# The last down block ahead of each later first up product is put 128 bytes further, in a longer tile

## The chip, the cores and the metric

The kernel runs on one core of one Trainium2 chip. The metric is the device time of one execution in microseconds, taken as the median of several runs; less is better. The profile shows one execution of the same program.

## The reference

One decoder block in fp32 on a sequence of 512 tokens of width 1024, in three residual parts and a final norm:

```python
h = rms_norm(x, g_mix);  proj = h @ w_in           # pooling mixer and differential attention, gated
x = x + mixed @ w_out
hc = rms_norm(x, g_cross)
x = x + memory_cross_attention(hc, mem_n, w_cq, w_ckv, w_co)
hm = rms_norm(x, g_mlp)                             # the part that this change touches
x = x + jnp.square(jax.nn.relu(hm @ w_up)) @ w_down # w_up 1024 x 4096, w_down 4096 x 1024
return rms_norm(x, g_final)
```

## The kernel before

Everything is kept transposed: features on the 128 partitions, tokens along the free dimension. Each fp32 product is made of three float32r matmuls (`mm3`, lines 105 to 107). Weights and right operands are split into hi, a copy rounded to float32r, and lo, what is left; the three matmuls are hi by hi, hi by lo, and lo by hi. Each loads its 128x128 weights anew (PEld in the profile) while the matmul before it streams. The split of a weight block of 128x1024 is a cast on ACT (line 111) and a subtraction on DVE (line 112).

Weights come in blocks of 128x1024 (512 KB). The list `blocks` holds them in the order of use. The MLP begins at block 64 (`FIRST_UP`) and has four groups of 22 blocks:

- 14 blocks for up products, in two sets of seven. The first matrix of the MLP is multiplied by a Strassen scheme (Winograd's form): seven block products of 256 columns in place of eight. Each is 24 matmuls 256 wide, `sc<-mix,...` or `sc<-s,...`, into PSUM tile `sc`, with right operands in the tiles `mix` and `s`. The first of a set is "A11", the second "s2" (in group 0's first set "s1").
- 8 blocks for down products. Each is 24 matmuls 512 wide, `acc<-xg,...`, into `acc`, with the right operand in `xg`. DVE then adds the result to the residual (line 573).

So group g uses the blocks from 64 + 22g on, and its last down block, number 64 + 22(g + 1) - 1, stands directly ahead of A11 of group g + 1. For groups 0, 1 and 2 these are blocks 85, 107 and 129, and the A11 behind them are blocks 86, 108 and 130.

In the MLP `weights(i)` loads blocks up to seven ahead and splits up to four ahead of block i. Splits go to buffers of two kinds. Blocks whose number leaves a remainder of 3 or 4 by 5 go to the tag `mhl`, which has four buffers, two pairs of hi and lo. All others go to `whi` and `wlo`, with three each. Together that is five blocks: the one in use and four ahead. The order of PE's instructions is the program's; the other engines' order is set by a scheduler, which also hands a buffer to a new tile once its last reader is done. Unsplit blocks lie in `wraw` (three) and `mraw` (five). Loads are issued by SP, and POOL issues those that add a second part of a weight onto a first; sums of parts are also made by DVE (lines 182 and 185).

Tiles of a tag lie one behind another. Where each begins in a partition follows from the sizes. Past a multiple of 512 bytes, `whi`, `wlo`, `xg` and the all-ones matrix `ones` begin at 0, `mhl` at 256, `mix` at 64 and `s` at 320; slices within them are multiples of 512 bytes.

During the third product of group 0, the row sums for the norm of the MLP (`stats2`) put two 512-wide matmuls on `ones` between the others (lines 237 and 238).

Of the kernel before, what the change touches and what calls it, by code (L numbers as in the profile page):

```python
# [12 lines left out]
F32R = mybir.dt.float32r  # L13
# [4 lines left out]
P = 128  # L18
T = 512
D = 1024  # L20
# [5 lines left out]
NG = FF // (P * KC)  # L26
# [24 lines left out]
def block_kernel(ctx: ExitStack, tc: tile.TileContext, x0g, xT, memT, wv, wm, wst, wckv, wpool, vecs, csts, outT):  # L51
# [17 lines left out]
    def nm(s):  # L69
        uid[0] += 1  # L70
        return f"{s}_{uid[0]}"
# [4 lines left out]
    def sb(tag, shape, bufs, dt=F32):  # L76
        p = apool if tag in EARLY_TAGS else late["pool"] if tag in LATE_TAGS else pool
        return p.tile(shape, dt, tag=tag, name=nm(tag), bufs=bufs)
# [16 lines left out]
    def f(ap):  # L95
        return ap.bitcast(F32)
# [13 lines left out]
    def split(hi, lo, src, eng=V):  # L110
        S.copy(hi, src)  # L111
        eng.tensor_tensor(lo, src, f(hi), op=ALU.subtract)  # L112
# [27 lines left out]
    def add(src):  # L140
        blocks.append(src)
        return len(blocks) - 1
# [12 lines left out]
    def load(i):  # L155
        if i >= len(blocks):
            return
        if isinstance(blocks[i], tuple):
            n, name = blocks[i]
            if (n, "A11") not in raw:  # L160
                fetch((n, "A11"), part(n, "A11"), "mraw", 5)
            if (n, "s1") not in raw and name in ("s1", "s2"):
                r = fetch((n, "s1"), part(n, "A22"), "wraw", 3)
                nc.gpsimd.dma_start(r, part(n, "A21"), accum_op=ALU.add)
            if (n, "s3") not in raw and name == "s3":
                r = fetch((n, "s3"), part(n, "A21"), "mraw", 5)
                nc.gpsimd.dma_start(r, part(n, "A11"), accum_op=ALU.add)  # L167
            if name in ("A12", "A22"):
                fetch((n, name), part(n, name), "mraw", 5)
        elif i == 0 and i not in raw:  # L170
            r = raw[i] = sb("wraw", [P, D], 3)
            nc.sync.dma_start(r[:, :T], blocks[i][:, :T])
            load_x(1)
            nc.sync.dma_start(r[:, T:], blocks[i][:, T:])
        else:
            fetch(i, blocks[i], "wraw", 3)

    def combined(n, name):

        if name == "s2":  # L180
            r = raw[n, "s2"] = sb("wraw", [P, D], 3)
            V.tensor_tensor(r, raw[n, "s1"], raw[n, "A11"], op=ALU.add)
        elif name == "s4":
            r = raw[n, "s2"]
            V.tensor_tensor(r, r, raw[n, "A12"], op=ALU.add)
            return r
        return raw[n, name]

    def prep(i):
        if i >= len(blocks) or i in ready:  # L190
            return
        load(i)
        r = combined(*blocks[i]) if isinstance(blocks[i], tuple) else raw[i]
        if i >= FIRST_UP and i % 5 > 2:
            hi = sb("mhl", [P, D], 4, F32R)
            lo = sb("mhl", [P, D], 4, F32R)
        else:
            hi = sb("whi", [P, D], 3, F32R)
            lo = sb("wlo", [P, D], 3, F32R)
        if i == 0:  # L200
            V.tensor_copy(hi[:, :T], r[:, :T])
            V.tensor_tensor(lo[:, :T], r[:, :T], f(hi[:, :T]), op=ALU.subtract)
            split(hi[:, T:], lo[:, T:], r[:, T:])
        else:
            split(hi, lo, r, G if i in WPOOL else V)
        ready[i] = (hi, lo)

    def weights(i):
        far = 4 if i >= FIRST_UP else 0
        for j in range(i, i + 4 + far):  # L210
            if j < FIRST_UP or late:
                load(j)
        for j in range(i, i + 3 + far // 2):
            if j < FIRST_UP or late:
                prep(j)
        return ready.pop(i)
# [104 lines left out]
    for m in CO_ORDER:  # L321
        where["co", m] = add(wm[WCO + m])
    FIRST_UP = len(blocks)
    for g in range(NG):
        for n in (2 * g, 2 * g + 1):
            for name in FIRST_ORDER if n == 0 else ORDER:
                where[n, name] = add((n, name))
        for m in range(KC):
            where["dn", g, m] = add(wm[WDN + KC * g + m])
# [19 lines left out]
    load(0)  # L349
    x_in(0)  # L350
    prep(0)
    x_in(1)
    for k in range(2, KC):
# [568 lines left out]
    for g in range(NG):  # L922
# [3 lines left out]
        for m in range(KC):  # L926
# [4 lines left out]
            if last and m == KC - 1:  # L931
                st["sp3"] = split_sq(ss3, T)
                for hf, o in enumerate((ps("sc", 3), ps("sc", 3))):
                    c = slice(hf * M, (hf + 1) * M)
# [90 lines left out]
```

## Time and profile before

| | |
|---|---|
| median of 3 runs | 734.94 us (733.79 to 735.09) |
| profiled execution, its own time | 733.65 us |
| its span, first to last instruction | 731.7 us |
| mean granted TensorE clock | 0.987 |
| busy: PE / PEld / DVE / ACT / POOL | 706.8 / 614.1 / 512.7 / 392.4 / 72.6 us |
| HBM read / written | 86.24 / 2.10 MB |

Busy time is the time in which an engine has an instruction under way. PE is the matmuls and PEld the weight loads, which overlap them; matmuls are pipelined, so the duration of one is longer than the step from its start to the next one's. A row of the timeline gives start in us, duration in us, engine, line, operation, out<-in and shape; in brackets stands the idle time ahead of it and what ended it.

### The profile page before, as it was taken

The page shows a single profiled execution, that of the slowest core. Times are in us where ns is not written, and L with a number is a line of the kernel's source. Part 1 is how long each engine was busy: PE and PEld are TensorE (multiplying, and loading weights), DVE is VectorE, ACT ScalarE, POOL GpSimd, SP SyncE. Part 2 cuts the span into 40 slices and gives each one's busy share as a digit, 9 for nine tenths or more (in the row PEclk, how much of TensorE's full clock was granted, in tenths as well). Part 3 has the DMA queues.
Part 4 walks back from the last instruction along what each step waited for, and adds up shares of the span by engine and source line. Part 5 has one row for each costly group of instructions (what it writes and reads, how often), then busy time and mean ns, then how long its engine had stood idle before and what let it go on. Part 6 is the DMA issues. An engine that isn't in the chain of part 4 may idle for free.

```text
span 731.7 us, 10275 instructions
## 1 busy us (share of the span) xinstructions
PE 706.8 (97%) x3960; PEld 614.1 (84%) x3960; DVE 512.7 (70%) x797; ACT 392.4 (54%) x641; POOL 72.6 (10%) x66
## 2 busy tenths in 40 slices
PE   9999999999999999999969999999999999999993
PEld 6877888788889888888849988899889988899882
DVE  7597999975888555663887974588455974489426
ACT  7498998676766433543754641256214651256422
POOL 0044112534000000000000001000000001000003
PEclk9999999999999999999988999999999999999997
DMA  8433223143525542114734646265354645314003
GB/s 318 142 114 117 78 82 115 59 142 119 173 91 186 187 141 87 58 58 159 187 86 122 197 143 144 86 173 184 77 115 146 202 144 118 83 58 144 30 1 115
DMA packets 28112, 91.09 MB, mean 124 GB/s; under 512 B 3072, under 2 KB 5120, under 8 KB 28064
## 3 DMA queue, kind: packets, MB, share of 16 engines
q1 hardware_dynamic: 25712, 81.92, 33.9%
q0 software_dynamic: 2352, 8.52, 6.9%
q8 instruction: 31, 0.51, 0.3%
q14 instruction: 17, 0.14, 0.1%
HBM read 86.24 MB, written 2.10 MB: 121 GB/s over the span
## 4 chain that ended last, share of the span: by engine, by line
PE 81%; DVE 6%; DMA 5%; ACT 5%; issue 1%; POOL 0%; SPq 0%; DVEq 0%; POOLq 0%; ACTq 0%
PE acc L105 16%; PE acc L107 15%; PE acc L106 15%; PE sc L105 10%; PE sc L107 10%; PE sc L106 10%; DMA wraw<-wst 3%; DMA mraw<-wst 2%; DVE wlo L112 1%; ACT tmp L448 1%; ACT whi L111 1%; DVE mix L849 1%; DVE tmp L446 1%; DMA tmp<-xT 1%; PE sc L387 1%
## 5 line engine op out<-in xcount | busy, mean ns | idle before, releaser
L111 ACT CAST whi<-wraw 128x1024 fp32r<-128x1024 f32 (+1 forms) x98 | 102.4, 1045 | 118.1 <-PE acc L106 50.8
L105 PE MATMUL acc<-xg,whi 128*128 128x512 f32 x400 | 158.2, 396 | 0.0
L107 PE MATMUL acc<-xg,wlo 128*128 128x512 f32 x400 | 156.1, 390 | 0.0
L106 PE MATMUL acc<-xg,whi 128*128 128x512 f32 x400 | 155.8, 390 | 0.0
L112 DVE TENSOR_TENSOR wlo<-wraw,whi 128x1024 fp32r<-128x1024 f32 (+1 forms) x98 | 121.3, 1238 | 27.7 <-ACT whi L111 27.4
L107 PEld LDWEIGHTS acc<-xg,wlo 128*128 128x128 f32 x400 | 75.1, 188 | 16.1
L105 PEld LDWEIGHTS acc<-xg,whi 128*128 128x128 f32 x400 | 75.2, 188 | 15.0 <-issue 0.3
L106 PEld LDWEIGHTS acc<-xg,whi 128*128 128x128 f32 x400 | 75.2, 188 | 14.5
L573 DVE TENSOR_TENSOR vr<-acc,vr 128x512 f32<-128x512 f32 x41 | 28.3, 690 | 72.3 <-PE acc L107 72.3
L105 PE MATMUL sc<-mix,whi 128*128 128x256 f32 (+1 forms) x192 | 56.8, 296 | 0.0
L107 PE MATMUL sc<-mix,wlo 128*128 128x256 f32 (+1 forms) x192 | 56.4, 294 | 0.0
L106 PE MATMUL sc<-mix,whi 128*128 128x256 f32 (+1 forms) x192 | 56.4, 294 | 0.0
L885 DVE TENSOR_TENSOR tmp<-sc,tmp 128x512 f32<-128x512 f32 x56 | 37.7, 686 | 7.5 <-PE sc L107 7.3
L111 ACT CAST mhl<-wraw 128x1024 fp32r<-128x1024 f32 x22 | 23.2, 1053 | 35.6 <-PE acc L106 22.2
L111 ACT CAST whi<-mraw 128x1024 fp32r<-128x1024 f32 x19 | 19.9, 1050 | 38.6 <-PE acc L106 21.8
L106 PE MATMUL acc<-xg,mhl 128*128 128x512 f32 x104 | 40.6, 390 | 0.0
L105 PE MATMUL acc<-xg,mhl 128*128 128x512 f32 x104 | 40.5, 389 | 0.0
L107 PE MATMUL acc<-xg,mhl 128*128 128x512 f32 x104 | 40.5, 389 | 0.0
L105 PEld LDWEIGHTS sc<-mix,whi 128*128 128x128 f32 x192 | 36.5, 190 | 1.0
L106 PEld LDWEIGHTS sc<-mix,whi 128*128 128x128 f32 x192 | 36.4, 189 | 1.1
L107 PEld LDWEIGHTS sc<-mix,wlo 128*128 128x128 f32 x192 | 36.4, 190 | 1.1
L167 POOL DMA_DIRECT2D mraw<-wst x8 | 6.9, 864 | 263.5 <-DMA mraw<-wst 164.3
(270 smaller groups left out, 1684.9 us busy)
## 6 DMA issues: line engine op xcount, KB each, us to landing
wraw<-wm SPq DMA_DIRECT2D x76, 512.0 KB, 3.3
mraw<-wst SPq DMA_DIRECT2D x32, 512.0 KB, 3.4
wraw<-wckv SPq DMA_DIRECT2D x16, 512.0 KB, 3.4
mraw<-wst POOLq DMA_DIRECT2D x8, 512.0 KB, 5.7
wraw<-wst SPq DMA_DIRECT2D x8, 512.0 KB, 3.3
wraw<-wst POOLq DMA_DIRECT2D x8, 512.0 KB, 5.6
s<-s SPq DMA_DIRECT2D x8, 256.0 KB, 3.6
vr<-xT SPq DMA_DIRECT2D x8, 256.0 KB, 4.4
```

Of the source, the lines that this page charges most:

```text
L105: nc.tensor.matmul(o, lh, rh, start=start, stop=False)
L106: nc.tensor.matmul(o, lh, rl, start=False, stop=False)
L107: nc.tensor.matmul(o, ll, rh, start=False, stop=stop)
L111: S.copy(hi, src)
L112: eng.tensor_tensor(lo, src, f(hi), op=ALU.subtract)
L167: nc.gpsimd.dma_start(r, part(n, "A11"), accum_op=ALU.add)
L387: nc.tensor.matmul(o[i], xg[k][0][:, tb], wh[:, c], start=k == 0, stop=False)
L446: V.tensor_tensor_reduce(e[:, :n], o[:, :n], mask[:, T - n:], -0.125, 3.0e38, ALU.add, ALU.min, mn)
L448: S.activation(e[:, :n], e[:, :n], AF.Exp, bias=mn, scale=-1.0, accum_out=sm[:, c:c + 1])
L573: V.tensor_tensor(t, o, t, op=ALU.add)
L849: eng.tensor_tensor(y3[j][:, i, c], y3[j][:, i, c], r, op=ALU.mult)
L885: V.tensor_tensor(u[new], o, u[old], op=ALU.add)
```

## The change

Two things change. All four `mhl` buffers are declared 32 elements (128 bytes) longer. The blocks 85, 107 and 129 (`LAST_DOWN`) take their hi and lo from `mhl` and use its elements 32 to 1055 in place of 0 to 1023. Blocks 85 and 107 were in `whi` and `wlo` before; 129 was in `mhl` already. All other `mhl` blocks use elements 0 to 1023 of the longer buffers. No instruction is added or removed, and nothing that is computed changes.

```diff
@@ prep
-        if i >= FIRST_UP and i % 5 > 2:
-            hi = sb("mhl", [P, D], 4, F32R)
-            lo = sb("mhl", [P, D], 4, F32R)
+        if i >= FIRST_UP and (i % 5 > 2 or i in LAST_DOWN):
+            c = slice(32, 32 + D) if i in LAST_DOWN else slice(D)
+            hi = sb("mhl", [P, D + 32], 4, F32R)[:, c]
+            lo = sb("mhl", [P, D + 32], 4, F32R)[:, c]
         else:
             hi = sb("whi", [P, D], 3, F32R)
             lo = sb("wlo", [P, D], 3, F32R)
@@ the list of blocks
     FIRST_UP = len(blocks)
+    LAST_DOWN = {FIRST_UP + 22 * (g + 1) - 1 for g in range(NG - 1)}
```

## The prediction

> **What bounds the kernel now.** I read the page first: busy times, the slices, the chain by engine.
>
> ```profile
> span 731.7 us, 10275 instructions
> ...
> PE 706.8 (97%) x3960; PEld 614.1 (84%) x3960; DVE 512.7 (70%) x797; ACT 392.4 (54%) x641; POOL 72.6 (10%) x66
> ...
> PE   9999999999999999999969999999999999999993
> ...
> PE 81%; DVE 6%; DMA 5%; ACT 5%; issue 1%; POOL 0%; SPq 0%; DVEq 0%; POOLq 0%; ACTq 0%
> ```
>
> PE is busy everywhere, and the chain is PE. The second view is PE's waits, longest first:
>
> ```profile
> PE sc L105 <- ACT mix L111: 4.0, 1, 4.0
> PE sc L106 <- DVE mix L112: 3.2, 1, 3.2
> ```
>
> These two are where the MLP begins (slice 21); no longer wait of PE is listed, so within the MLP PE waits for nobody that matters. What can move there is the spacing of matmuls. So the third view is busy time by stretch; I cut it at the first matmul of each stage. A row gives the length in us, then PE's, the weight loads', DVE's, ACT's and POOL's busy time, the granted clock, the DMA share and GB/s.
>
> ```profile
> 396.82:424.02 27.20, 27.20 (x242) 27.20 (x241) 26.20 (x35) 17.77 (x24) 0.85 (x1) 1.00 0.65 184
> 467.78:507.36 39.58, 39.58 (x338) 39.58 (x336) 32.96 (x40) 22.77 (x28) 0.86 (x1) 1.00 0.56 173
> 550.91:590.49 39.58, 39.58 (x337) 39.57 (x336) 32.95 (x40) 22.77 (x28) 0.86 (x1) 1.00 0.57 173
> 634.05:673.62 39.57, 39.57 (x337) 39.57 (x336) 32.95 (x40) 22.76 (x28) 0.00 (x0) 1.00 0.28 93
> 435.14:467.78 32.64, 32.64 (x145) 27.03 (x144) 15.06 (x15) 6.32 (x7) 2.58 (x3) 1.00 0.48 113
> ```
>
> The first row is ten 256-wide up products of group 0, 240 matmuls: 27.20/240 = 113.3 ns from one to the next. The next three are all 14 up products of groups 1, 2 and 3, 336 matmuls each: 39.58/336 = 117.8 ns. Same shape, same code, same clock (1.00), PE busy throughout, yet 4.46 ns apart, and constant within each stretch. The last row is six 512-wide down products, 144 matmuls at 226.7 ns. So the up products have a quick and a slow pace, and something at the entry picks one. The fourth view, the timeline of PE, shows the entries: the only change to quick in the MLP, and an entry into slow.
>
> ```profile
> 394.20 0.28 PE L107 MATMUL sc<-mix,wlo 128*128 128x256 f32 x1
> 394.32 0.40 PE L237 MATMUL tr<-tmp,ones 128*128 128x512 f32 x1
> 394.56 0.39 PE L238 MATMUL tr<-tmp,ones 128*128 128x512 f32 x1
> 394.78 0.28 PE L105 MATMUL sc<-mix,whi 128*128 128x256 f32 x1
> 394.90 0.28 PE L106 MATMUL sc<-mix,whi 128*128 128x256 f32 x1
> 395.01 0.28 PE L107 MATMUL sc<-mix,wlo 128*128 128x256 f32 x1
> ...
> 467.55 0.39 PE L107 MATMUL acc<-xg,wlo 128*128 128x512 f32 x1
> 467.78 0.28 PE L105 MATMUL sc<-mix,whi 128*128 128x256 f32 x1
> 467.90 0.28 PE L106 MATMUL sc<-mix,whi 128*128 128x256 f32 x1
> 468.02 0.28 PE L107 MATMUL sc<-mix,wlo 128*128 128x256 f32 x1
> ```
>
> Two 512-wide matmuls on `ones` in the middle of a product (the row sums of `stats2`) turn 0.12 us steps into 0.11; a full down block ahead of A11 leaves 0.12. The pace is a state that the last wide matmuls hand on, and the change touches exactly the block that hands it on to groups 1, 2 and 3.
>
> That the place of the operands matters to spacing at all is seen in two other products, each of 24 matmuls, whose weights and right operand lie otherwise to each other:
>
> ```profile
> 249.64 0.40 PE L105 MATMUL acc<-whi,s 128*128 128x512 f32 x1
> 255.24 0.40 PE L105 MATMUL acc<-whi,s 128*128 128x512 f32 x1
> ...
> 711.74 0.28 PE L105 MATMUL sc<-xg,whi 128*128 128x256 f32 x1
> 714.61 0.28 PE L105 MATMUL sc<-xg,whi 128*128 128x256 f32 x1
> ```
>
> Tiles begin, past a multiple of 512 bytes: `whi`, `wlo`, `xg`, `ones` at 0, `mhl` at 256, `mix` at 64, `s` at 320 (from the tiles' sizes in order). With weights in `s` and the right side in `whi`, 512-wide: 5.60/24 = 233.3 ns, not 226.7. With `whi` and `xg`, 256-wide: 2.87/24 = 119.6, not 113.3 or 117.8.
>
> **The change part by part.** No instruction is added or removed.
>
> (1) *Shifted last block.* Blocks 85, 107, 129 have their weights 128 bytes further, so the A11 products of groups 1 to 3 are entered from another relation. No row has a 128-byte shift: known are 0 and 256 (down blocks from `whi` and `mhl`, equal below) and 64 (unequal above). Bounds: all three groups turn quick, 3 x 336 x 4.46 ns = 4.50 us gained; or none, 0. I take the gain. The quick pace once entered held for all ten remaining products of group 0, over every change of tile, and the slow one over 14, so the entry decides; and a block of 24 matmuls with two shifted loads out of three is a larger disturbance than the two on `ones`. Against: `ones` is itself at offset 0, so what turned the pace there was not an offset.
>
> (2) *Longer tiles.* The four `mhl` buffers are 4224 bytes apart, not 4096, so they begin at 256, 384, 0 and 128 past 512. As the buffers are handed out, every `mhl` block's hi stays on a multiple of 256 and its lo lies 128 off; in the three shifted blocks hi is off and lo is not.
>
> ```profile
> L106 PE MATMUL acc<-xg,whi 128*128 128x512 f32 x152 | 59.1, 389 | 0.0
> L106 PE MATMUL acc<-xg,mhl 128*128 128x512 f32 x104 | 40.6, 390 | 0.0
> L107 PE MATMUL sc<-mix,mhl 128*128 128x256 f32 x88 | 25.2, 287 | 0.0
> L107 PE MATMUL sc<-s,mhl 128*128 128x256 f32 x88 | 24.5, 278 | 0.0
> ```
>
> (The 287 holds a stretch at half clock at the start of the MLP.) In up products 88 + 88 = 176 lo matmuls move; in down products (104/8 = 13 blocks now, 15 after) 12 x 8 lo and 3 x 16 hi, 144. Bounds: nothing, as between 0 and 256 bytes above (389 and 390 ns each); or the dearest rows, 176 x (119.6 - 113.3) = 1.1 us and 144 x (233.3 - 226.7) = 1.0 us, 2.1 us together. A gain on the wide ones is excluded: 226.7 is the lowest spacing they show. I take 0.5 us, near the row of the nearest shift.
>
> (3) *Buffers.* Blocks 85 and 107 leave `whi`/`wlo` (three each) for `mhl` (two pairs): 85 waits for 83's pair, 109 for 107's.
>
> ```profile
> 456.92 1.05 ACT L111 CAST mhl<-wraw 128x1024 fp32r<-128x1024 f32 x1 [4.43 <-PE acc L106]
> 458.00 1.22 DVE L112 TENSOR_TENSOR mhl<-wraw,mhl 128x1024 fp32r<-128x1024 f32 x1 [0.21 <-ACT mhl L111]
> 462.34 0.39 PE L105 MATMUL acc<-xg,whi 128*128 128x512 f32 x1
> ...
> 550.89 1.05 ACT L111 CAST whi<-mraw 128x1024 fp32r<-128x1024 f32 x1 [4.34 <-PE acc L106]
> 551.11 0.69 DVE L573 TENSOR_TENSOR vr<-acc,vr 128x512 f32<-128x512 f32 x1 [3.31 <-PE acc L107]
> 551.97 1.22 DVE L112 TENSOR_TENSOR wlo<-mraw,whi 128x1024 fp32r<-128x1024 f32 x1 [0.16 <-ACT whi L111]
> 553.74 0.28 PE L105 MATMUL sc<-s,mhl 128*128 128x256 f32 x1
> ```
>
> 83 ends near 456.9, where today 88 takes its pair: 85 would be ready at 458.00 + 1.22 = 459.2 and is wanted at 462.34, 3.1 us spare. 107 ends near 550.9, where today 112 is split: 109 would be ready at 551.97 + 1.22 = 553.19, wanted at 553.74, 0.55 us spare. Behind those waits on ACT and DVE stand only later splits and the residual adds, which come first on DVE (551.11); the raw tiles of 85 and 109 are held some 16 us longer, and SP's and POOL's loads into them are wanted groups of products later. Cost 0. If ACT put one more 1.05 us cast first at 550.89, PE would wait about 0.5 us, once. Blocks 86, 87, 90, 110 to 112 get buffers sooner, which nobody awaits.
>
> The sum, against the profiled execution (731.7 span, 733.65 with what lies around it): -4.50 + 0.5 = -4.0. The median of the runs is 734.94, 1.29 above that execution; I take the change off the median: 734.94 - 4.50 + 0.5 = 730.9.
>
> **The rivals.** *No effect:* the pattern of places repeats every 128 bytes, or the pace hangs on how the last wide matmuls end and not on addresses. For it: `ones` above, and `whi` against `mhl` equal. Against: 64 bytes matter. Time 734.9.
> The Trainium skill ("TensorE: Matmul & The Clock Gate", Part 2, Step-by-step) speaks for this one: PE reads the moving operand and the next weights over two independent ports, so loading weights takes no bandwidth from a running matmul. By that rule no placement costs and the time is unchanged; the trace agrees where 389 and 390 ns stand side by side, and does not where 119.6, 117.8 and 113.3 do.
>
> *Part of the groups turn:* group 2's A11 has its weights in `mhl`, groups 1 and 3 in `whi`, so entries differ; or a `mhl` product within a group, its lo now 128 off, throws the pace back. One group quick: 734.94 - 1.50 + 0.5 = 733.9; two: 732.4.
>
> *Slower:* the lo's of the longer tiles are the wrong relation. Place: 37 `mhl` blocks. Price: up to 2.1 us, and group 0 loses its quick pace, (424.02 - 394.78)/0.1133 = 258 matmuls x 4.46 ns = 1.15 us. With no group turning that is 738.2. It decides from 1.5 us, say group 0's loss plus 50 of the 320 moved matmuls at 6.6 ns. For it: the paces above never improve on 113.3 and 226.7, and both were reached with hi and lo alike. Against: a shift of 256 costs nothing.
>
> **How the numbers follow.** 0.2% of 734.94 is 1.5 us, about what a measurement of this kernel can tell from no change. Chances: all three turn 0.36; part 0.12; no effect 0.32; slower 0.20. Faster: 0.36 and half of the partial ones, 0.42. Within 0.2%: the no-effect case and the other half, 0.38. Slower 0.20. Predicted is the likeliest, 730.9; its own range is 729.6 (all gained, nothing paid, a run 0.8 below) to 732.6 (the full 2.1 paid). The range over all reaches from 729.6 over the unchanged time to 736.7, which leaves out half of the slower case and the tail of the first.
>
> **What would show it.** Right: the up stretches of groups 1, 2 and 3 take 38.1 us each, not 39.6, with the clock at 1.00; group 0's ten products stay at 27.2; wide `mhl` products stay at 226.7 ns; no wait of PE at the first s2 of group 2. Wrong: stretches of 39.6 (no effect); stretches that change pace at a `mhl` product (partial); group 0 above 27.2 or wide products towards 233 (slower).

## The result and the profile after

| | before | after |
|---|---|---|
| median of 12 runs | 735.21 us (733.79 to 736.65) | 737.32 us (736.09 to 739.61) |
| profiled execution, its span | 731.7 us | 734.3 us |
| ratio of the times, 95% interval | | 1.0024 [1.0014, 1.0034] |

The change makes the kernel slower by 0.24%, above the range of the prediction and on the other side of its forecast. Line numbers are two higher in the changed kernel from the list of blocks on: the residual add is line 575. The rows below are of its page: the groups of the wide down products from `mhl`, with busy time, mean ns of one, and idle time ahead.

```profile
L107 PE MATMUL acc<-xg,mhl 128*128 128x512 f32 x120 | 47.7, 397 | 0.0
L106 PE MATMUL acc<-xg,mhl 128*128 128x512 f32 x120 | 47.6, 397 | 0.0
...
L105 PE MATMUL acc<-xg,mhl 128*128 128x512 f32 x120 | 46.9, 391 | 0.0
```

Before, line 106 from `mhl` took 390 ns on average; now it and line 107 take 397. The busy time by stretch of the changed kernel shows it block by block. The columns are those of the prediction.

```profile
396.41:423.61 27.20, 27.20 (x242) 27.20 (x241) 26.19 (x35) 17.50 (x24) 0.85 (x1) 1.00 0.64 182
440.24:445.68 5.44, 5.44 (x25) 4.51 (x24) 2.49 (x3) 1.05 (x2) 0.00 (x0) 1.00 0.50 87
451.12:456.67 5.55, 5.55 (x25) 4.54 (x24) 1.92 (x2) 1.03 (x1) 0.00 (x0) 1.00 0.85 189
462.22:467.83 5.61, 5.61 (x25) 4.51 (x24) 1.92 (x2) 1.08 (x2) 0.86 (x1) 1.00 0.59 93
467.83:507.57 39.74, 39.74 (x338) 39.74 (x337) 34.09 (x42) 22.77 (x28) 0.86 (x1) 1.00 0.58 173
535.02:541.24 6.22, 5.60 (x26) 4.35 (x24) 1.97 (x3) 1.82 (x2) 0.00 (x0) 1.00 0.53 84
552.40:592.13 39.73, 39.73 (x337) 39.73 (x336) 34.23 (x41) 22.72 (x28) 0.86 (x1) 1.00 0.60 173
636.18:675.89 39.71, 39.71 (x337) 39.70 (x336) 33.01 (x40) 22.77 (x28) 0.00 (x0) 1.00 0.30 93
```

- Row 1: group 0's ten up products stay quick, 27.20 us.
- Rows 2 to 4: a down block from `whi` takes 5.44 us, one from `mhl` with its lo 128 bytes off 5.55, and block 85, which is shifted, 5.61.
- Rows 5, 7 and 8: the up products of groups 1 to 3 take 39.74, 39.73 and 39.71 us, 0.14 to 0.16 more than before. None turned quick.
- Row 6: block 105 in group 2 takes 6.22 us, of which PE is busy 5.60. That is a wait, the only one that is listed within the MLP:

```profile
PE acc L105 <- DVE vr L575: 0.6, 1, 0.6
```

The timeline of PE shows where in a product the time goes (start in us, duration, engine, line):

```profile
523.92 0.39 PE L105 MATMUL acc<-xg,mhl 128*128 128x512 f32 x1
524.15 0.40 PE L106 MATMUL acc<-xg,mhl 128*128 128x512 f32 x1
524.38 0.40 PE L107 MATMUL acc<-xg,mhl 128*128 128x512 f32 x1
524.62 0.39 PE L105 MATMUL acc<-xg,mhl 128*128 128x512 f32 x1
```

Three matmuls take 0.70 us; from `whi` they take 3 x 226.7 = 680 ns. In the trace's start times in ns, the step after line 105 stays at 227, that after line 106 (during which the lo is loaded) is 232 to 233, and that after line 107 (which uses the lo) 234 to 235.

The wait has its cause on DVE. The timeline of DVE in the changed kernel around it (idle time and its releaser in brackets):

```profile
539.27 1.22 DVE L182 TENSOR_TENSOR wraw<-wraw,mraw 128x1024 f32<-128x1024 f32 x1 [7.52 <-DMA wraw<-wst]
540.41 0.68 DVE L575 TENSOR_TENSOR vr<-acc,vr 128x512 f32<-128x512 f32 x1
541.01 1.22 DVE L112 TENSOR_TENSOR mhl<-mraw,mhl 128x1024 fp32r<-128x1024 f32 x1
542.14 0.69 DVE L575 TENSOR_TENSOR vr<-acc,vr 128x512 f32<-128x512 f32 x1
```

and the same place in the kernel before:

```profile
534.79 0.69 DVE L573 TENSOR_TENSOR vr<-acc,vr 128x512 f32<-128x512 f32 x1 [3.16 <-PE acc L107]
...
540.23 0.69 DVE L573 TENSOR_TENSOR vr<-acc,vr 128x512 f32<-128x512 f32 x1 [2.10 <-PE acc L107]
...
542.39 1.22 DVE L182 TENSOR_TENSOR wraw<-wraw,mraw 128x1024 f32<-128x1024 f32 x1
```

The scheduler has put a sum of weight parts (line 182) ahead of the residual add in place of behind it. DVE stands idle for 7.52 us until a transfer lands, and behind that sum stands the add that frees the PSUM tile for PE.

Summed product by product over the MLP, up to the first narrow product behind it (711.74 us before, 714.32 after): wide `mhl` products +1.64 us; 17 narrow `mhl` products in the slow pace, 2.853 for 2.827 us each, +0.45; blocks 105 and 106 of group 2 +0.89; the second product of the MLP, whose mean granted clock was 0.91 after and 0.78 before, 3.09 for 3.54, -0.45; the start of that product +0.05. That is +2.58, the whole difference between the two profiled executions (the medians differ by 2.11). The -0.45 is not the change's: in `no_107` below, whose instructions up to there are the same in kind and order, that product took 3.62 us.

### The profile page after: what moved, and what is told of

It is laid out like the page before. It is cut to its first block, busy times and chain, and to the rows that moved or that the text cites. A ratio compares the mean times of both kernels' runs of the same rounds, so it can differ in the third digit from the quotient of the medians.

```text
span 734.3 us, 10273 instructions
## 1 busy us (share of the span) xinstructions
PE 708.4 (96%) x3960; PEld 615.0 (84%) x3960; DVE 512.1 (70%) x797; ACT 392.2 (53%) x641; POOL 72.6 (10%) x66
## 5 line engine op out<-in xcount | busy, mean ns | idle before, releaser
L111 ACT CAST whi<-wraw 128x1024 fp32r<-128x1024 f32 (+1 forms) x96 | 100.2, 1044 | 116.0 <-PE acc L106 44.4
L105 PE MATMUL acc<-xg,whi 128*128 128x512 f32 x384 | 152.2, 396 | 0.6 <-DVE vr L575 0.6
L107 PE MATMUL acc<-xg,wlo 128*128 128x512 f32 x384 | 150.0, 391 | 0.0
L106 PE MATMUL acc<-xg,whi 128*128 128x512 f32 x384 | 149.7, 390 | 0.0
L112 DVE TENSOR_TENSOR wlo<-wraw,whi 128x1024 fp32r<-128x1024 f32 (+1 forms) x96 | 119.0, 1240 | 26.4 <-ACT whi L111 26.0
L107 PEld LDWEIGHTS acc<-xg,wlo 128*128 128x128 f32 x384 | 72.1, 188 | 15.4
L105 PEld LDWEIGHTS acc<-xg,whi 128*128 128x128 f32 x384 | 72.2, 188 | 15.1 <-issue 1.0
L106 PEld LDWEIGHTS acc<-xg,whi 128*128 128x128 f32 x384 | 72.3, 188 | 13.9
L107 PE MATMUL acc<-xg,mhl 128*128 128x512 f32 x120 | 47.7, 397 | 0.0
L106 PE MATMUL acc<-xg,mhl 128*128 128x512 f32 x120 | 47.6, 397 | 0.0
L111 ACT CAST mhl<-wraw 128x1024 fp32r<-128x1024 f32 x24 | 25.3, 1053 | 41.9 <-PE acc L106 28.1
L105 PE MATMUL acc<-xg,mhl 128*128 128x512 f32 x120 | 46.9, 391 | 0.0
```

What stands on the lines that cost most here:

```text
L105: nc.tensor.matmul(o, lh, rh, start=start, stop=False)
L106: nc.tensor.matmul(o, lh, rl, start=False, stop=False)
L107: nc.tensor.matmul(o, ll, rh, start=False, stop=stop)
```

## The experiments

Three theories stood after this. *Place*: the relation of the weights' address to that of the right operand sets the step, and the longer tiles put every lo of `mhl` into a dearer one. *Order*: the move of a block changed the scheduler's order on DVE. *Pair*: the pace of the up products is turned by two wide matmuls amid narrow ones, not by an address.

### Where the time went: long_only, move_only, no_107, shift_129

`long_only` has the longer tiles alone; no block is moved or shifted.

```diff
-            hi = sb("mhl", [P, D], 4, F32R)
-            lo = sb("mhl", [P, D], 4, F32R)
+            hi = sb("mhl", [P, D + 32], 4, F32R)[:, slice(D)]
+            lo = sb("mhl", [P, D + 32], 4, F32R)[:, slice(D)]
```

> The longer mhl tiles alone: no block is moved or shifted, the buffers lie 4224 bytes apart, so that every lo in mhl begins 128 bytes off a multiple of 256. Theory of the place (a weight load 128 off costs about 6.7 ns in the matmul that it loads under and in the one that it runs in): the 13 wide mhl blocks take 5.55 us instead of 5.44 (1.4 us together), the 16 mhl up products of groups 1 to 3 2.853 instead of 2.826 (0.43 us), group 0's stay at 2.72, no wait of PE in the MLP, the whole 1.8 us slower than before. Rival, theory of the buffers (the loss comes from blocks 85 and 107 changing their buffers): no difference from before.

Measured: 736.01 against 734.15 us, ratio 1.0027 [1.0012, 1.0041]. Its groups of PE:

```profile
L107 PE MATMUL acc<-xg,mhl 128*128 128x512 f32 x104 | 41.3, 397 | 0.0
L106 PE MATMUL acc<-xg,mhl 128*128 128x512 f32 x104 | 41.3, 397 | 0.0
L105 PE MATMUL acc<-xg,mhl 128*128 128x512 f32 x104 | 40.5, 389 | 0.0
```

The 397 of the changed kernel are there, with no block shifted: 5.547 us for a wide `mhl` product, 2.853 for a narrow one in the slow pace, 2.720 still in the quick. Summed over the MLP, +1.23 wide and +0.45 narrow: 1.68 us, and no wait of PE. The longer tiles alone carry most of the loss: 1.86 us by the medians, of 2.11 for the whole change.

`move_only` moves blocks 85 and 107 to `mhl`, with tiles of the old length and no shift.

```diff
-        if i >= FIRST_UP and i % 5 > 2:
+        if i >= FIRST_UP and (i % 5 > 2 or i in LAST_DOWN):
...
```

> Blocks 85 and 107 take their buffers from mhl as in the changed kernel, but tiles keep their length and nothing is shifted. Theory of the buffers: DVE puts the sum of parts of L182 ahead of a residual add in group 2, PE waits about 0.6 us for that add and the two blocks around it take about 0.9 us more; every other product as before; the whole 0.9 us slower. Rival, theory of the place: no difference from before, and the wait goes away with the longer tiles.

Measured: 734.14 against 734.15 us, ratio 0.9997 [0.9980, 1.0014]. Wide products from `mhl` take 5.44 us again. DVE's timeline has the new order:

```profile
537.81 1.23 DVE L182 TENSOR_TENSOR wraw<-wraw,mraw 128x1024 f32<-128x1024 f32 x1 [6.63 <-DMA wraw<-wst]
538.95 0.68 DVE L575 TENSOR_TENSOR vr<-acc,vr 128x512 f32<-128x512 f32 x1
```

but blocks 105 and 106 lose only 0.13 us together (5.453 and 5.560 us), not 0.89. The order is the move's; its price depends on when the transfer lands, here 6.63 and not 7.52 us after DVE began to wait.

`no_107` is the changed kernel with block 107 left in `whi` and `wlo`.

```diff
-    LAST_DOWN = {FIRST_UP + 22 * (g + 1) - 1 for g in range(NG - 1)}
+    LAST_DOWN = {FIRST_UP + 22 * (g + 1) - 1 for g in (0, 2)}
```

> The changed kernel, but block 107 stays in whi and wlo unshifted; 85 moves and is shifted as before, and so is 129. Theory of the buffers (the wait in group 2 comes from 107's change, by which DVE's order puts L182 and its wait for a transfer ahead of a residual add): no wait of PE in group 2, its wide whi blocks all at 5.44; what remains is the cost of places, 1.8 us and twice 0.06. Rival (the wait comes from 85, or from the longer tiles): the wait of about 0.6 us is still there.

Measured: 738.77 us in one run, median of before 734.93. DVE's old order is back:

```profile
544.14 0.69 DVE L575 TENSOR_TENSOR vr<-acc,vr 128x512 f32<-128x512 f32 x1 [2.11 <-PE acc L107]
...
546.31 1.23 DVE L182 TENSOR_TENSOR wraw<-wraw,mraw 128x1024 f32<-128x1024 f32 x1
```

and with it the wait is gone: all `whi` blocks of group 2 take 5.440 us. It is the move of 107 that reorders DVE. Yet the run as a whole is slow, for three reasons that lie ahead of the first instruction that the edit changes: the MLP began 1.9 us later than in the changed kernel (377.37 for 375.46), its second product took 0.53 us longer, and group 0 stayed in the slow pace, which costs 1.25 us from the pair of `stats2` on. The last is taken up below.

`shift_129` has tiles 64 elements longer, which keeps all of `mhl` on multiples of 256 bytes, and shifts block 129 alone.

```diff
+            c = slice(32, 32 + D) if i == FIRST_UP + 65 else slice(D)
-            hi = sb("mhl", [P, D], 4, F32R)
+            hi = sb("mhl", [P, D + 64], 4, F32R)[:, c]
... (lo alike)
```

> mhl tiles are 256 bytes longer, so that all buffers begin on a multiple of 256 again, and of the last down blocks only 129 is shifted by 128 bytes, hi and lo alike; no block changes its kind of buffer. Theory of the place: block 129 takes 24 x 6.7 ns more, 5.60 us instead of 5.44, every other block as before, and the first product behind it stays slow, 2.83 us. Rival 1 (only a difference between hi and lo costs): block 129 stays at 5.44. Rival 2 (a block shifted as a whole does turn the pace): group 3's 14 up products take 2.72 us each, 38.1 in all, instead of 39.6.

Measured: 733.33 us in one run, median of before 734.15. Its busy time by stretch, for block 128, block 129 and the up products of group 3:

```profile
622.59:628.03 5.44, 5.44 (x25) 4.50 (x24) 3.14 (x3) 1.06 (x1) 0.00 (x0) 1.00 0.06 12
628.03:633.62 5.59, 5.59 (x25) 4.53 (x24) 1.92 (x2) 1.08 (x2) 0.00 (x0) 1.00 0.29 97
633.62:673.20 39.58, 39.58 (x338) 39.58 (x337) 32.95 (x40) 22.76 (x28) 0.00 (x0) 1.00 0.26 94
```

The shifted block itself pays 0.15 us, its `mhl` neighbour nothing, and the up products behind it stay at 117.8 ns. The shift alone is a small loss in the trace, too small to be seen in one run's time, and it turns nothing.

### What turns the pace: the pairs

`ones_mid` puts two 512-wide matmuls on `ones` into A11 of groups 1 to 3, after 12 of its 24; what they compute is not read.

```diff
+    def turn(again):
+        t = ps("tr", 2)
+        nc.tensor.matmul(t, ones, again[0], start=True, stop=False)
+        nc.tensor.matmul(t, ones, again[1], start=False, stop=True)
...
+                if again and i == 0 and k == 3:
+                    turn(again)
```

> The kernel before with two 512-wide matmuls on ones, into a PSUM tile that nobody reads, put into A11 of groups 1, 2 and 3 after its fourth of eight steps, the way the row sums stand in group 0. Theory of the interruption (two wide matmuls in the middle of a slow product turn the pace, whatever the places): after them the products take 2.72 us, the up stretches of groups 1 to 3 shrink from 39.6 to about 38.7 us each with the 0.46 us of the two added, the whole 2.7 us faster than before. Rival (group 0 is quick for another cause, such as the half clock ahead of it): the products stay at 2.83, the whole is 1.4 us slower.

Measured: 731.74 against 734.15 us, ratio 0.9960 [0.9943, 0.9977]. A11 takes 3.242 us and the 13 products behind it 2.720 each; the stretch of group 1, with the two in it, is shorter than the 39.58 us of before:

```profile
467.65:506.25 38.60, 38.60 (x339) 38.51 (x338) 32.56 (x40) 22.81 (x28) 0.86 (x1) 1.00 0.55 179
```

Two added matmuls make the kernel faster: each group pays 3.242 - 2.827 = 0.415 us and gets 13 x 0.107 = 1.39 back.

Three variants ask what it takes: one of the two (`ones_one`), the two ahead of A11, behind the down block's last matmul (`ones_edge`), and the two only 256 wide (`ones_narrow`).

```diff
 ones_one
-        nc.tensor.matmul(t, ones, again[0], start=True, stop=False)
-        nc.tensor.matmul(t, ones, again[1], start=False, stop=True)
+        nc.tensor.matmul(t, ones, again[0], start=True, stop=True)
 ones_edge
...
+            if again and name == "A11":
+                turn(again)
             block_product(w, right[RIGHT[name]], o)
 ones_narrow
+        nc.tensor.matmul(t[:, :M], ones, again[0][:, :M], start=True, stop=False)
+        nc.tensor.matmul(t[:, :M], ones, again[1][:, :M], start=False, stop=True)
```

> As the kernel with two wide matmuls on ones inside A11 of groups 1 to 3, but with one of the two. Theory of the interruption, if any wide matmul amid slow narrow ones will do: quick pace after it, up stretches of 38.1 + 0.2 to 0.3 = 38.4 us instead of 38.6, the whole 0.6 us faster than with two. Rival (it takes two: the first is entered late, 241 ns, and only the second hands on an early start, 224 ns): pace stays slow, up stretches 39.8, the whole 0.7 us slower than before.

> The same two wide matmuls on ones, but between the last down block and A11, so that they come after wide matmuls and not amid narrow ones. Theory of the interruption (what counts is the change from narrow to wide and back within two matmuls): pace stays slow, each up stretch 39.6 + 0.45 us. Rival (the weights in ones, or that the last two loads are of one tile, turn the pace): quick after it, 38.1 + 0.45 us.

> As the kernel with two wide matmuls on ones inside A11 of groups 1 to 3, but the two are 256 wide. Theory of the interruption, if the width is what counts: slow as before, up stretches 39.6 + 0.24 = 39.8 us. Rival (it is the change of tiles that counts, the right operand in xg at a multiple of 512 instead of mix): quick after them, 38.1 + 0.24 = 38.4 us.

Measured: `ones_one` 735.52 against 735.62 us, ratio 1.0006 [0.9993, 1.0020]; `ones_edge` 735.53 us in one run (median of before 735.62); `ones_narrow` 734.45 in one run (734.93). In all three the products behind A11 stay at 2.827 us. Two wide matmuls behind a block that is wide already do not turn the pace. One wide matmul does not, and two narrow ones do not, at the place where the pair of `ones_mid` does. In all three groups that is the same place, behind 12 narrow matmuls, and `hold_phase` below shows that the place counts; at another one they were not tried.

`hold_two` adds nothing. Of the last down block ahead of each A11 it holds back the last two matmuls (hi by lo and lo by hi) and issues them after 12 of A11's 24.

```diff
...
+    def release(held):
+        (o, hi, lo, r), m = held
+        nc.tensor.matmul(o, hi, r[1], start=False, stop=False)
+        nc.tensor.matmul(o, lo, r[0], start=False, stop=True)
+        finish(m, o, False)
...
+                if held and i == 0 and k == 3:
+                    release(held)
```

> The kernel before, with the last two matmuls of the last down block of groups 0, 1 and 2 (hi by lo and lo by hi of its last step) held back and issued inside the next A11 after its fourth of eight steps, instead of two added ones. Nothing is computed twice or left out; the residual add comes 1.4 us later. Theory of the interruption (two wide matmuls amid slow narrow ones turn the pace, on whatever weights): quick after them, A11 with the two and the down block ahead together at 8.25 us against 8.27, up stretches without A11 at 13 x 2.72 = 35.4 us instead of 36.75, the whole 4.2 us faster than before, about 1.5 us faster than with the two on ones. Rival (it needs one and the same weight tile twice, as with ones): slow as before, no difference.

Measured: 731.30 against 734.93 us, ratio 0.9950 [0.9930, 0.9969]; the lowest ratio of all versions, though its interval overlaps that of `ones_mid`. Its busy time by stretch, for the last ten up products of group 0 and for all 14 of group 1 (groups 2 and 3 take 38.60 us as well):

```profile
397.26:424.46 27.20, 27.20 (x242) 27.20 (x241) 26.19 (x35) 17.64 (x24) 0.86 (x1) 1.00 0.64 183
467.80:506.40 38.60, 38.60 (x339) 38.51 (x338) 32.58 (x40) 22.84 (x28) 0.86 (x1) 1.00 0.61 176
```

38.60 us now holds two wide matmuls more than the 39.58 of before. Per group: the down block is shorter by 0.454 us, A11 longer by 0.415, 13 products shorter by 0.107: -1.43, three times -4.29 (the medians differ by -3.63; the interval reaches from -5.1 to -2.3). The pair in group 1, from PE's timeline:

```profile
469.10 0.28 PE L107 MATMUL sc<-mix,wlo 128*128 128x256 f32 x1
469.22 0.40 PE L873 MATMUL acc<-xg,whi 128*128 128x512 f32 x1
469.46 0.39 PE L874 MATMUL acc<-xg,wlo 128*128 128x512 f32 x1
469.68 0.28 PE L105 MATMUL sc<-mix,whi 128*128 128x256 f32 x1
469.79 0.28 PE L106 MATMUL sc<-mix,whi 128*128 128x256 f32 x1
```

The steps are 0.24 and 0.22 us (241 and 224 ns in the trace), then 0.11.

`hold_phase` issues the pair one matmul later in group 1, two later in group 2 and three later in group 3.

```diff
+                if held and i == 1 and k == 0:
+                    oo, (h, l), (rh, rl) = o[:, M:], (w[0][:, e], w[1][:, e]), rhs[0]
+                    for j, (a, b) in enumerate(((h, rh), (h, rl), (l, rh))):
+                        nc.tensor.matmul(oo, a, b, start=j == 0, stop=False)
+                        if j == held[2]:
+                            release(held)
+                    continue
```

> As the kernel that holds back the last two matmuls of the down block, but they are issued one matmul later in group 1, two later in group 2 and three later in group 3 (after 13, 14 and 15 narrow matmuls of A11 instead of 12). The slow pace repeats every three matmuls (118, 117, 118 ns and so on). Theory of the phase (the two wide ones turn the pace only if they come at the right step of the three): group 3, a full three later, is quick, 13 products at 2.72 us behind A11; at least one of groups 1 and 2 stays slow, 2.83 us. Rival (any place amid slow narrow matmuls will do): all three quick.

Measured: 732.41 us against 735.36, one run each. Group 1 turns (steps of the pair 230 and 224 ns, products behind at 2.720 us), group 3 turns (241 and 224), group 2 does not (230 and 231, products at 2.827). Group 2's pair:

```profile
551.93 0.40 PE L884 MATMUL sc<-mix,mhl 128*128 128x256 f32 x2
552.16 0.39 PE L873 MATMUL acc<-xg,whi 128*128 128x512 f32 x1
552.39 0.39 PE L874 MATMUL acc<-xg,wlo 128*128 128x512 f32 x1
552.62 0.28 PE L884 MATMUL sc<-mix,mhl 128*128 128x256 f32 x1
```

Three later is again as none later, which fits a step of three; but each of the three places was tried once, each in another group. (The `mhl` weights of group 2's A11 are not what kept it slow, since `hold_two` turned that group.) In the MLP, 20 pairs of wide matmuls came into a slow narrow stream at plus or minus 64 bytes in the profiles of this case. The second step was 224 or 225 ns in 18 of them, and all 18 turned quick; it was 231 in the other two, and they stayed slow. So a second step of 224 is the mark of a turn to quick there. That the place in the program isn't the whole of it is seen in group 0, where the pair of `stats2` stands after the same six matmuls of the same product in every kernel (it is the fourth product, A12; the text ahead of the prediction calls it the third). In the changed kernel it turned the pace (steps 230 and 224):

```profile
393.92 0.39 PE L238 MATMUL tr<-tmp,ones 128*128 128x512 f32 x1
394.15 0.39 PE L239 MATMUL tr<-tmp,ones 128*128 128x512 f32 x1
394.37 0.28 PE L105 MATMUL sc<-mix,whi 128*128 128x256 f32 x1
```

and in `no_107` it did not (230 and 231):

```profile
396.22 0.39 PE L238 MATMUL tr<-tmp,ones 128*128 128x512 f32 x1
396.45 0.39 PE L239 MATMUL tr<-tmp,ones 128*128 128x512 f32 x1
396.68 0.28 PE L105 MATMUL sc<-mix,whi 128*128 128x256 f32 x1
```

In `ones_narrow` group 0 had begun quick, and the same pair turned it slow (steps 231 and 236); in `mix192` it had begun quick too, and the pair left it so (232 and 233). What the step of three counts from, at the start of the MLP, stays open.

A pair of wide matmuls is not the only thing that turns the pace. Ahead of the MLP, near 221 us, two 512-wide matmuls on `ones` stand in a narrow stream of the memory attention as well (right operand `s`, weights `whi` and `wlo`). In three of the 14 profiles (the kernel before, `no_107`, `shift_129`) the pace turned quick there, in `mix192` it turned slow, and in the others neither. In `no_107` and `shift_129` the quick pace ended 24 narrow matmuls later at one long step of 138 ns with no wide matmul near, here in `shift_129`:

```profile
224.36 0.28 PE L107 MATMUL acc<-s,wlo 128*128 128x256 f32 x1
224.47 0.30 PE L105 MATMUL acc<-s,whi 128*128 128x256 f32 x1
224.61 0.28 PE L106 MATMUL acc<-s,whi 128*128 128x256 f32 x1
```

In the kernel before, a step of 140 ns at the same place left the pace quick. So a break in the even steps can turn the pace too, and whether it does is not settled by the program alone.

### Whether the place sets the step: mix128, mix192

`mix128` moves `mix` and `s` by 64 bytes, `mix192` by 128, by the size of small tiles ahead of them.

```diff
 mix128
-        ... sb("mrstd", [P, w + 48], 1)[:, :w]
+        ... sb("mrstd", [P, w + 32], 1)[:, :w]
-        few = sb("lam", [P, 16], 1)
+        few = sb("lam", [P, 32], 1)
 mix192
+        ... sb("mrstd", [P, w + 16], 1)[:, :w]
+        few = sb("lam", [P, 48], 1)
```

> The kernel before with mix and s 64 bytes further: they begin at 128 and 384 past a multiple of 512, so the narrow products' right operand lies 128 from its weights by 256 and not 64; all other tiles as before. Theory of the place (what counts is weights against right operand, by 256 bytes): the spacing of all narrow products in the MLP changes, and does so alike for whi and mhl; by the 6.7 ns steps seen so far 113.3, 117.8 or 120 ns, that is stretches of 38.1, 39.6 or 40.3 us. Rival (the place of the weights alone counts): no change, 117.8 in groups 1 to 3.

> The kernel before with mix and s 128 bytes further, at 192 and 448 past a multiple of 512. By the theory of the place this is the relation that the lo loads of mhl had to mix and s in the changed kernel (weights 64 ahead of the right operand instead of 64 behind), now for all loads: 6.7 ns more per matmul than quick, 120 ns, and no quick pace in group 0: stretches of 40.3 us, 2 us slower in the up products. Rival (only weights count): no change.

Measured, one run each, median of before 735.62: `mix128` 739.01 us, with the narrow products of groups 1 to 3 at 2.880 us (120 ns) and those of group 0 at 2.845 to 2.851 (118.5 to 118.8 ns), without the quick pace of 113.3; `mix192` 734.53 us, with both paces as before (2.720 and 2.827), so the 120 ns expected of it did not come. In wide products elsewhere `mix192` changed two values in opposite directions: the out-projection (weights in `whi`, right side in `mix`) went from 5.494 to 5.600 us, and a product of the memory attention (weights in `s`, right side in `whi`) from 5.600 to 5.494. The rows of `mix128` are those of the last ten up products of group 0 and of the 14 of group 1:

```profile
398.74:427.22 28.48, 28.48 (x242) 28.48 (x241) 26.79 (x35) 17.51 (x24) 0.85 (x1) 1.00 0.62 183
470.76:511.07 40.31, 40.31 (x337) 40.31 (x336) 33.13 (x41) 22.71 (x28) 0.86 (x1) 1.00 0.56 170
```

Where all loads of a stream lie alike, the values of these runs fit one table, by the weights' offset less the right operand's, past a multiple of 256 bytes:

| offset | 512 wide | 256 wide |
|---|---|---|
| 0 | 226.7 ns | 119.6 to 120 ns |
| -64 | 228.9 | 113.3 or 117.8 |
| +64 | 233.3 | 113.3 or 117.8 |
| 128 | 232.1 to 233.3 | 118.5 to 120 |

The place theory holds, with a period of 256 bytes, for the four offsets that were tried; others were not. The quick pace of 113.3 ns was seen at plus and minus 64 only. At 128 there were two values as well, 118.5 to 118.8 ns in group 0 and 120.0 behind it, at a granted clock of 1.00 in both. Why narrow and wide matmuls prefer different offsets is not settled.

## Why the prediction was wrong, step by step

**Step 1, the shifted last block, failed.** It took -4.50 us for "the entry decides" by the operands' place. In the changed kernel all three entries stayed slow, and `shift_129` shows the same for a shift alone: 0 of 4.50 gained, 0.15 to 0.17 us lost in each shifted block. What it had right is that the pace is a state that is kept over products; what it had wrong is what sets it. The objection that it wrote down itself, that `ones` lies at offset 0, was the answer: two wide matmuls between slow narrow ones turn the pace (`ones_mid`, `hold_two`), at two of the three places tried (`hold_phase`), and a full wide block ahead does not (before; `ones_edge` with two more). What the state consists of stays open. Its "larger disturbance" of 24 matmuls is no disturbance of the narrow stream at all, since it ends before the stream begins.

**Step 2, the longer tiles, was mis-sized.** Taken 0.5 us "near the row of the nearest shift", that of 256 bytes; measured 1.64 + 0.45 = 2.09 us, at the bound of 2.1. The row at 256 said nothing of 128, since 256 is the period; the rows at 64 bytes that showed a dearer step were the ones to take. The bound's parts were less exact than their sum: 1.0 was put down for the wide products, and 1.64 was measured, since the matmul under which the lo is loaded pays as well as the one that uses it; 1.1 for the narrow, and 0.45 was measured, since the quick ones pay nothing and the slow ones 0.027 us per product.

**Step 3, the buffers, at no cost, failed in a small term.** The spare times were right as far as they went: at block 109, with 0.55 us to spare, PE does not wait. But "the residual adds, which come first on DVE" was read off the order of before, at 551 us alone, and the move of 107 changed that order 11 us ahead of it: a sum that waits for a transfer now stands ahead of a residual add, at 0.13 us (`move_only`) to 0.89 us (the changed kernel).

**The rivals.** *No effect* had half of it: the pace does not hang on the last block's address. Beside it the prediction put the Trainium skill's rule of two independent read ports ("TensorE: Matmul & The Clock Gate", Part 2, Step-by-step), by which a weight load takes no read bandwidth from a running matmul. That no placement costs, as the prediction drew from it, the runs here contradict: with the load 128 bytes off, the matmul it runs under takes 232 to 233 ns, not 227. Whether it is read bandwidth that is lost, no run shows. *Slower* named the right mechanism, place and price (the longer tiles, 2.1 us), but added the loss of group 0's quick pace, which the changed kernel kept (27.20 us) and `no_107` lost. With 2.1 us and without that loss its time would have been 737.0, 0.3 below the measured median. That closeness is partly luck: the wait of 0.89 us is in none of its terms, and the second product's -0.45 took half of it off in the profiled execution. *Part of the groups turn* did not come: no up product of groups 1 to 3 turned quick.

## What to carry to other kernels

Before operands are shifted, list the step between matmuls of every pair of tiles in the trace against the difference of their addresses, and bound an unseen offset by the dearest row, not by the nearest in bytes when that may be a whole period. Where two stretches of equal work run at two constant steps, look at what turned one into the other and put just that in again with harmless work: one such test (`ones_mid`) would have told more than the address did, and led to a version, `hold_two`, that is 0.5% faster by issuing two matmuls later at each of three places. A block that changes buffers changes the order of a scheduled engine too: look for a wait on a transfer that may come to stand ahead of what frees PSUM.

## What was not expected of the hardware

- The step of a 512-wide float32r matmul with a weight load for each goes from 226.7 to 233.3 ns with the offset of weights against right operand, with a period of 256 bytes (`mix192`).
- The same narrow products run at 113.3 or 117.8 ns for hundreds of matmuls at the full granted clock, and two 512-wide matmuls between them can change the one into the other, in both directions (`hold_two`, `ones_narrow`), and so can one long step of 138 ns (`shift_129`).
- Work added on the bounding engine made the kernel faster: six wide matmuls, ratio 0.9960 [0.9943, 0.9977].
